# The opening's pair product by channel tiles, all tokens in a step

## The chip, the core and the metric

The kernel runs on one core of a Trainium2 chip. The metric is the device time of one execution in microseconds, as the median of several runs; the profile is of one execution more. The engines have short names: PE (TensorE) multiplies matrices and transposes, ACT (ScalarE) applies functions and copies, DVE (VectorE) does element-wise arithmetic, POOL (GpSimd) here only issues transfers that add into memory, and SP issues the ordinary transfers.

## The reference

A trunk of two layers on x (512 tokens, 1024 channels, float32), each layer a gated feed-forward block, a token mixer, and a second feed-forward block. The change touches the first feed-forward block of the first layer alone:

```python
def rms_norm(x, g):
    y = xf * lax.rsqrt(jnp.mean(xf * xf, axis=-1, keepdims=True) + NORM_EPS)
    return (y * g)
def swiglu(x, w_in, w_out):
    g, u = jnp.split(x @ w_in, 2, axis=-1)          # w_in: 1024 x 5632
    return (jax.nn.silu(g) * u) @ w_out             # w_out: 2816 x 1024
for i in range(DEPTH):                              # DEPTH = 2
    h = h + 0.5 * swiglu(rms_norm(h, ffn1_norm[i]), ffn1_w_in[i], ffn1_w_out[i])
    ...                                             # mixer, then a second feed-forward block
return rms_norm(h, final_norm)
```

## The kernel before

**Products in three parts.** Every operand is split into a high part (`hi`, `whi`) and the rest (`lo`, `wlo`), and a product is made of three matmuls: high by high, low by high, high by low. ACT rounds to the high part (line 96), DVE subtracts to get the rest (line 87; line 93 where a gain is applied at once). Rounded weights lie in four buffers (`whi`, `wlo`), the weights as loaded in eight (`raw`, 1024 columns each).

**The row norm.** The input of the feed-forward block is not divided by its row norm. x is transposed on PE (line 265, tile `e`), multiplied by the channel gain, and used so; the factor `rt` per token is applied to the product, inside the silu and in the product after it. It needs the squares of x (`junk`, ACT), a mean (DVE), a root (ACT) and a Newton step (DVE). The norm is therefore not needed until the first silu.

**Units of x.** x falls into four quarters, A11, A12, A21 and A22 (first digit: tokens 0 to 255 or 256 to 511; second: channels 0 to 511 or 512 to 1023), and each quarter into two groups of 256 channels (`first.g[0]` and `first.g[1]`). A quarter of one group is called a unit here: 256 tokens by 256 channels. A unit is turned by four transposes (`turn`), split (`parts`: two `hi` on ACT, two `lo` on DVE) and kept as a value (`value`) for sums.

**Steps.** The work is a list of steps (`subs`); a step is 12 or 24 matmuls with one weight tile. The list is walked in order (lines 1423 to 1439). Each step has places called pre, mid and rest, before its matmuls, and end and late, after them; `hook(n, place, function)` puts work there. Weights are split some steps ahead, by a table `ahead` in the opening, by three steps later. All instructions of an engine run in the order in which this walk writes them.

**The opening.** Steps 0 to 7 are the pair product, `pair_plain` with `first`: gate and up columns of two blocks (2 x 256 columns) for all tokens, into four PSUM banks (`p`), two for each half of the tokens. Steps 0 to 3 do the first half of the tokens (A12, then A11, a group each), steps 4 to 7 the second half (A22, then A21) with the same four weight tiles of 256 channels by 512 columns, which are held in the four buffers. Silu and the gated product `h` come at steps 7 to 9, which frees the banks. Steps 8 to 21 are the first `chunk` (line 673), a product by a scheme of seven products over quarters and their sums: P1 (A11), P2 (A12), P5 (S1), P6 (S2), P3 (S4), P7 (S3), Q4 (A22), two steps each, into banks A (of `bank`), B (of the pool `aux`) and C. P5, at step 12, is the first to need the two banks C, which the pair product's `h` has to free. `first.rest` puts the sums S1 to S3 and their splits at steps from 5 on. The results are transposed to be the left side of the next product: the pair group's from step 15 on (`left_blocks` with lag 7), the chunk's at the ends of steps 18, 19, 22 and 23. From step 22 on follows the product with w_out (`out_blocks`), whose update is `x<-A,x`.

**Transfers.** SP issues x and the opening's weights: two units of x (256 KB each), the first weight tile in two halves, the second, a quarter of x (512 KB), two weight tiles, two quarters, then the chunk's weights. POOL's adding transfers follow for the weights of P5 and P7.

Of the kernel before, what the change touches and what calls it, by code (L numbers as in the profile page):

```python
# [9 lines left out]
F32R = mybir.dt.float32r  # L10
# [3 lines left out]
P = 128  # L14
# [38 lines left out]
def trunk(ctx: ExitStack, tc: tile.TileContext, a: dict, out: bass.AP):  # L53
# [29 lines left out]
    def f32(t):  # L83
        return t.bitcast(F32)
# [26 lines left out]
    class Raw:  # L111


        halves = False

# [34 lines left out]
    class Sub:  # L150
# [19 lines left out]
        def split(self, vector=False):  # L170

# [549 lines left out]
    def pair_plain(w_in, f0, group, first=False):  # L721


        w, st, ht = 2 * P, {}, {}
        raw = {}
        for k in (1, 0):
            for h in range(2):
                raw[k, h] = PairRaw(w_in, k * 512 + h * 256, f0)
                raws.append(raw[k, h])

        def bank_of(half, s):
            if (half, s) not in st:
                st[half, s] = bank("p")
            return st[half, s]

        def product(sub, half, left, h, between=None):

            sq = [(s, q) for q in range(2) for s in range(2)]
            for i, (s, q, m) in enumerate([(s, q, m) for m in range(3) for s, q in sq] if first and h else
                                          [(s, q, m) for q in range(2) for m in range(3) for s in range(2)] if first else  # L740
                                          [(s, q, m) for s, q in sorted(sq) for m in range(3)]):
                if i == 8 and between is not None:
                    between()
                z = S.z[h].hl[left][m == 1][:, q * H + s * P : q * H + (s + 1) * P]
                nc.tensor.matmul(bank_of(half, s), z, (sub.lo if m == 2 else sub.hi)[:, q, :],  # L745
                                 start=left[2] == "2" and (h, q, m) == (0, 0, 0),
                                 stop=left[2] == "1" and (h, q, m) == (1, 1, 2))

        def silu(half, s):
            t = 2 * half + s  # L750
            ht[t] = slot(name="s1")[:, :w]
            act(ht[t], st[half, s][:, :w], AF.Silu, scale=S.rt[:, t : t + 1])

        def post(half):
            for s in range(2):
                ps, t = st[half, s], 2 * half + s
                if t not in ht:
                    silu(half, s)
                o = slot(name="h")[:, :w]
                stt(o, ps[:, w:], S.rt[:, t : t + 1], ht[t], ALU.mult, ALU.mult)  # L760
                ht[t] = o
            left_blocks(group, ht, half, 7 if first else 2)

        at0 = len(subs)
        for i, (half, left) in enumerate(((0, "A12"), (0, "A11"), (1, "A22"), (1, "A21"))):
            for h in range(2):
                def mm(sub, half=half, left=left, h=h):
                    product(sub, half, left, h, opening["A11"] if first and (left, h) == ("A12", 1) else None)

                end = None  # L770
                if (left, h) == ("A11", 1):
                    end = (lambda: (hook(at0 + 7, "rest", lambda: (silu(0, 0), silu(0, 1))),
                                    hook(at0 + 8, "mid", lambda: post(0)))) if first else lambda: post(0)
                elif (left, h) == ("A21", 1):
                    end = (lambda: hook(at0 + 9, "rest", lambda: post(1))) if first else lambda: post(1)
                subs.append(Sub(raw[1 - i, h], mm, end) if i < 2 else Again(subs[at0 + 2 * (i - 2) + h], mm, end))

    class PairRaw(Raw):


        def __init__(self, w_in, r0, f0):
            super().__init__(None, [P, 2, 512])
            self.w_in, self.r0, self.f0 = w_in, r0, f0

        def fetch(self):
            for q in ((slice(0, 1), slice(1, 2)) if self.halves else (slice(0, 2),)):
                for b, base in enumerate((0, DFF)):
                    c0 = base + self.f0 * P
                    ws = self.w_in[self.r0 + q.start * P : self.r0 + q.stop * P, c0 : c0 + 256]
                    nc.sync.dma_start(out=self.v[:, q, b * 256 : (b + 1) * 256],  # L790
                                      in_=ws.rearrange("(k p) c -> p k c", p=P))

    def ffn(w_in, w_out, norm):
        f0 = 0
        for i, sizes in enumerate(FF_PARTS):
            groups, p0 = [], f0
            for n in sizes:
                if n == "p":
                    groups.append(Group(1))
                    pair_plain(w_in, f0, groups[-1], not subs)  # L800
# [569 lines left out]
    def turn(i, name, where=None):  # L1370
        src, _ = first.src(i, name)
        opening[i, name] = first.g[i].turn(src, where)

    def parts(i, name):
        first.g[i].direct(name, opening[i, name], first.src(i, name)[1])

    def value(i, name, vector=False):

        g, ps, gains = first.g[i], opening.pop((i, name)), first.src(i, name)[1]
        if name == "A21" or not vector:  # L1380
            g.take(name, ps, gains)
            return
# [5 lines left out]
    turn(0, "A12")  # L1388
    warm_up(2, 512)
    turn(1, "A12")  # L1390
    warm_up(2, 512)
    parts(0, "A12")
    subs[0].split()
    parts(1, "A12")
    subs[1].split()
    value(0, "A12")
    value(1, "A12")
    opening["A11"] = lambda: (turn(0, "A11"), turn(1, "A11"))
    for n, phase, fn in ((0, "late", vec_rest),
                         (2, "pre", lambda: (subs[2].split(True), parts(0, "A11"), parts(1, "A11"))),  # L1400
                         (2, "pre", lambda: (subs[3].split(), value(0, "A11", True), value(1, "A11", True))),
                         (2, "end", lambda: (turn(0, "A22", bank), turn(1, "A22", bank))),
                         (3, "pre", lambda: (parts(0, "A22"), parts(1, "A22"))),
                         (3, "mid", lambda: (value(0, "A22"), value(1, "A22", True))),
                         (3, "end", lambda: (turn(0, "A21"), turn(1, "A21"))),
                         (4, "mid", lambda: (parts(0, "A21"), parts(1, "A21"))),
                         (4, "rest", lambda: (value(0, "A21"), value(1, "A21")))):
        hook(n, phase, fn)
    squares(4, "rest", "A11")
# [56 lines left out]
```

## Time and profile before

| | us |
|---|---|
| median of 3 runs | 1625.99 (1625.77 to 1626.8) |
| the profiled execution | 1628.51 |
| its span, first to last instruction | 1626.5 |
| mean granted TensorE clock in it | 0.997 |

| engine | busy us | share of the span | instructions |
|---|---|---|---|
| PE, matmuls | 1611.2 | 99% | 7451 |
| DVE | 1368.9 | 84% | 1830 |
| ACT | 1039.8 | 64% | 1511 |
| POOL | 222.5 | 14% | 201 |

Times in the profile count from the start of the span. A row of a timeline gives the start, the busy time, the engine, the line, the operation with its output and inputs, the shapes, the number of instructions merged into the row, and in brackets the idle time of the engine ahead of it with what ended that. A row of the windows gives the stretch and its length, the busy time of PE, PE's weight loads, DVE, ACT and POOL (with counts), the granted clock, the busy share of the transfer engines and their GB/s. A row of the chain of waits gives start, length and the work that the end of the execution hung on.

### The profile page before, as it was taken

How to read it: one execution, taken by the hardware profiler on the slowest of the kernel's cores; microseconds unless marked ns; L12 is line 12 of the kernel's file. 1: busy time of each engine (PE TensorE's matmuls, PEld its weight loads, DVE VectorE, ACT ScalarE, POOL GpSimd, SP SyncE). 2: the span in 40 equal slices, each digit the busy share in tenths (PEclk: the TensorE clock that was granted, in tenths of full speed). 3: DMA queues.
4: the chain of work that ended last, by engine and by line, in shares of the span. 5: the costliest groups of instructions: out<-in, count | busy, mean ns of one | idle time of the engine just before them, and what ended most of it. 6: DMA issues, size and time to landing. Idle time of an engine off the chain costs nothing.

```text
span 1626.5 us, 20830 instructions
## 1 busy us (share of the span) xinstructions
PE 1611.2 (99%) x7451; PEld 1328.9 (82%) x7451; DVE 1368.9 (84%) x1830; ACT 1039.8 (64%) x1511; POOL 222.5 (14%) x201
## 2 busy tenths in 40 slices
PE   9999999999999999999999999999999999999998
PEld 7888888888878888888888888888888788888886
DVE  6898888887898787877987978878978988879778
ACT  7656556657876656556776565566886765565665
POOL 2111111100010111111101111111211011111110
PEclk9999999999999999999999999999999999999999
DMA  8867876844383786876838778768877557686693
GB/s 273 188 164 166 209 179 158 217 119 115 83 204 84 175 202 162 208 174 158 202 86 190 173 161 211 181 151 209 214 196 193 155 117 195 161 208 162 159 207 99
DMA packets 164551, 279.29 MB, mean 172 GB/s; under 512 B 11504, under 2 KB 37728, under 8 KB 164448
## 3 DMA queue, kind: packets, MB, share of 16 engines
q1 hardware_dynamic: 114944, 184.84, 36.2%
q0 software_dynamic: 47712, 91.30, 33.6%
q10 hardware_dynamic: 1792, 1.84, 0.4%
q8 instruction: 58, 0.95, 0.2%
q14 instruction: 45, 0.37, 0.1%
HBM read 275.84 MB, written 2.10 MB: 171 GB/s over the span
## 4 chain that ended last, share of the span: by engine, by line
PE 90%; DVE 6%; ACT 3%; issue 1%; DMA 1%; SPq 0%; DVEq 0%; ACTq 0%
PE A L365 14%; PE A L366 14%; PE A L367 14%; PE C L366 7%; PE C L367 7%; PE C L365 7%; PE p L745 5%; PE B L365 4%; PE B L367 4%; PE B L366 4%; PE e L265 3%; PE Q L367 1%; PE Q L365 1%; PE Q L366 1%; DVE wlo L87 1%
## 5 line engine op out<-in xcount | busy, mean ns | idle before, releaser
L96 ACT ACTIVATE whi<-raw 128x1024 fp32r<-128x1024 f32 (+1 forms) x536 | 553.0, 1033 | 381.6 <-PE A L366 106.9
L87 DVE TENSOR_TENSOR wlo<-raw,whi 128x1024 fp32r<-128x1024 f32 (+1 forms) x537 | 638.9, 1193 | 182.3 <-ACT whi L96 181.0
L365 PE MATMUL A<-whi,hi 128*128 128x512 f32 x1016 | 405.4, 399 | 1.8 <-DVE x L93 1.8
L366 PE MATMUL A<-whi,lo 128*128 128x512 f32 x1016 | 397.7, 391 | 0.4 <-DVE lo L87 0.3
L367 PE MATMUL A<-wlo,hi 128*128 128x512 f32 x1016 | 397.8, 392 | 0.0
L367 PEld LDWEIGHTS A<-wlo,hi 128*128 128x128 f32 x1016 | 191.3, 188 | 41.7 <-DVE wlo L87 0.3
L366 PEld LDWEIGHTS A<-whi,lo 128*128 128x128 f32 x1016 | 191.7, 189 | 39.5 <-DVE lo L87 1.8
L365 PEld LDWEIGHTS A<-whi,hi 128*128 128x128 f32 x1016 | 191.3, 188 | 39.6 <-ACT whi L96 2.2
L366 PE MATMUL C<-whi,lo 128*128 128x512 f32 x560 | 219.2, 392 | 0.7 <-DVE lo L87 0.5
L365 PE MATMUL C<-whi,hi 128*128 128x512 f32 x560 | 218.8, 391 | 0.0
L367 PE MATMUL C<-wlo,hi 128*128 128x512 f32 x560 | 218.3, 390 | 0.0
L137 POOL DMA_DIRECT2D raw<-in_ffn_w_in_dram x82 | 98.8, 1205 | 741.9 <-DVE raw L87 524.9
L137 POOL DMA_DIRECT2D raw<-in_ffn_w_out_dram x72 | 83.0, 1160 | 378.8 <-DMA raw<-in_ffn_w_out_dram 124.3
L87 DVE TENSOR_TENSOR raw<-raw,raw 128x1024 f32<-128x1024 f32 (+1 forms) x108 | 129.6, 1200 | 1.2 <-DMA raw<-in_ffn_w_out_dram 0.6
L366 PEld LDWEIGHTS C<-whi,lo 128*128 128x128 f32 x560 | 105.2, 188 | 25.3 <-DVE lo L87 3.9
L87 DVE TENSOR_TENSOR lo<-a,hi 128x512 fp32r<-128x512 f32 (+1 forms) x188 | 122.7, 661 | 3.2 <-ACT hi L96 2.8
L96 ACT ACTIVATE hi<-a 128x512 fp32r<-128x512 f32 (+1 forms) x188 | 112.3, 601 | 19.3 <-DVE a L87 15.5
L365 PEld LDWEIGHTS C<-whi,hi 128*128 128x128 f32 x560 | 105.2, 188 | 21.8
L367 PEld LDWEIGHTS C<-wlo,hi 128*128 128x128 f32 x560 | 105.2, 188 | 21.6
L96 ACT ACTIVATE c<-A 128x512 f32<-128x512 f32 x132 | 77.3, 594 | 56.3 <-PE A L367 56.0
L365 PE MATMUL B<-whi,hi 128*128 128x512 f32 x280 | 112.2, 401 | 0.0
L367 PE MATMUL B<-wlo,hi 128*128 128x512 f32 x280 | 109.5, 391 | 0.0
(161 smaller groups left out, 2106.9 us busy)
## 6 DMA issues: line engine op xcount, KB each, us to landing
raw<-in_ffn_w_in_dram SPq DMA_DIRECT2D x162, 512.0 KB, 4.5
raw<-in_ffn_w_out_dram SPq DMA_DIRECT2D x100, 512.0 KB, 5.3
raw<-in_ffn_w_in_dram POOLq DMA_DIRECT2D x82, 512.0 KB, 7.5
raw<-in_ffn_w_out_dram POOLq DMA_DIRECT2D x60, 512.0 KB, 8.0
raw<-in_sg_w_in_dram SPq DMA_DIRECT2D x20, 512.0 KB, 6.6
raw<-in_rec_w_in_dram SPq DMA_DIRECT2D x16, 512.0 KB, 3.9
raw<-in_ffn_w_in_dram SPq DMA_DIRECT2D x30, 256.0 KB, 4.8
raw<-in_sg_w_in_dram POOLq DMA_DIRECT2D x12, 512.0 KB, 7.7
```

What stands on the lines that cost most here:

```text
L87: nc.vector.tensor_tensor(out=o, in0=x, in1=y, op=op)
L96: nc.scalar.activation(out=o, in_=x, func=f, **k)
L137: nc.gpsimd.dma_start(out=self.v, in_=src, accum_op=ALU.add)
L265: nc.tensor.transpose(ps[:, o : o + P], src(q, s), ident)
L365: nc.tensor.matmul(ps, zh, wh, start=fresh and i == 0, stop=False, **k)
L366: nc.tensor.matmul(ps, zl, wh, start=False, stop=False, **k)
L367: nc.tensor.matmul(ps, zh, wl, start=False, stop=end, **k)
L745: nc.tensor.matmul(bank_of(half, s), z, (sub.lo if m == 2 else sub.hi)[:, q, :], start=left[2] == "2" and (h, q, m) == (0, 0, 0), stop=lef ...
```

## The change

The opening's eight steps are written anew (`pair_opening`); other pair products keep the plain order.

- **Order of the product.** Step n takes one tile of 128 channels (tiles 4 to 7, then 0 to 3) for all 512 tokens: six matmuls for the first half of the tokens, six for the second. Each weight tile is 128 channels by 512 columns (256 KB, two transfers) and is used in its step only. So eight weight tiles are split, one each step, where four were held.
- **Order of the loads.** Unit n of x (256 KB) and weight tile n are issued in turn, n from 0 to 7; the units go A12, A22 of the first group, A12, A22 of the second, then A11, A21 of the first and of the second.
- **Inside a step** (`between`). After the first two matmuls of step n come the turn of unit n + 1, its `hi` and `lo`, the split of weight tile n + 1 and the value of unit n - 1. One warm-up pair of matmuls goes.
- **Splits ahead.** `ahead` is 0 to 4 at steps 0 to 4, 6 at step 5, 8 at step 6, 9 at step 7: so at step 6 the splits of weight tiles 7 and 8 (the chunk's first, 1024 columns) are written ahead of that step's `between`.
- **Later work.** Squares move from steps 4 to 6 to steps 5 to 8, the mean and root from step 6 to step 8 and the Newton step from 7 to 9, the four silus to step 9, the four products `h` to step 10, `first.rest` from 1 to 5, so that S1's splits are at steps 9 and 10. The pair group's transposes move from steps 15, 16, 16 and 17 to 17, 18, 19 and 20, and its sums with them from 19, 20 and 21 to 22, 23 and 24.
- **DVE and ACT.** The option that let DVE round a weight tile (line 184) goes; ACT rounds all.

The diff, cut to its core:

```diff
-        def split(self, vector=False):
+        def split(self):
...
-            for q in ((slice(0, 1), slice(1, 2)) if self.raw.halves else (slice(0, k),)):
-                if vector:
-                    nc.vector.tensor_copy(self.hi[:, q, :], src[:, q, :])
-                else:
-                    act(self.hi[:, q, :], src[:, q, :], AF.Copy)
-                tt(self.lo[:, q, :], src[:, q, :], f32(self.hi[:, q, :]), ALU.subtract)
+            act(self.hi, src, AF.Copy)
+            tt(self.lo, src, f32(self.hi), ALU.subtract)
...
+    def pair_opening(w_in, f0, group):
+        ps, ht = {}, {}
+        def mm_of(n, k):
+            def mm(sub):
+                c, h, q = k // 4, k % 4 // 2, k % 2
+                for half in range(2):
+                    name = ("A11", "A12", "A21", "A22")[2 * half + c]
+                    for m in range(3):
+                        for s in range(2):
+                            if n == 0 and m == 0:
+                                ps[half, s] = bank("p")
+                            z = S.z[h].hl[name][m == 1][:, q * H + s * P : q * H + (s + 1) * P]
+                            nc.tensor.matmul(ps[half, s], z, (sub.lo if m == 2 else sub.hi)[:, 0, :],
+                                             start=(n, m) == (0, 0), stop=(n, m) == (7, 2))
+                        if (half, m) == (0, 0):
+                            opening["between"](n)
+            return mm
+        for n, k in enumerate((4, 5, 6, 7, 0, 1, 2, 3)):
+            raws.append(PairRaw(w_in, k * P, f0, 1))
+            subs.append(Sub(raws[-1], mm_of(n, k)))
+        def out(half):
+            for s in range(2):
+                pair_out(ps[half, s], 2 * half + s, ht)
+            left_blocks(group, ht, half, 7 + 2 * half)
+        hook(9, "rest", lambda: [pair_silu(ps[t // 2, t % 2], t, ht) for t in range(TT)])
+        hook(10, "mid", lambda: out(0))
+        hook(10, "rest", lambda: out(1))
...
-    raws[0].halves = True
-    load_x(0, 512, 256)
-    load_x(0, 768, 256)
-    load_more(2)
-    load_x(0, 0)
-    load_more(4)
-    load_x(2, 512)
-    load_x(2, 0)
+    UNITS = [(i, name) for c in (1, 0) for i in range(2) for name in (("A11", "A21"), ("A12", "A22"))[c]]
+    for n, (i, name) in enumerate(UNITS):
+        load_x(QUARTER[name][0], QUARTER[name][1] * 512 + i * 256, 256)
+        load_more(n + 1)
...
+    HOME = (aux, aux, bank, bank, aux, aux, bank, aux)
...
+    def between(n):
+        if n == 0:
+            turn(1)
+            parts(1, 0)
+            subs[1].split()
+            parts(1, 1)
+        elif n < 7:
+            turn(n + 1)
+            parts(n + 1, 0, 1)
+            subs[n + 1].split()
+            value(n - 1)
...
-    squares(4, "rest", "A11")
-    squares(5, "rest", "A12")
-    squares(6, "rest", "A22")
-    squares(6, "rest", "A21")
-    rstd(6, (0, "rest"), (0, "rest"), (1, "pre"))
-    first.rest(1, None)
+    turn(0)
+    warm_up(2, 512)
+    parts(0, 0)
+    subs[0].split()
+    parts(0, 1)
+    hook(0, "late", vec_rest)
+    hook(7, "pre", lambda: value(6))
+    hook(7, "mid", lambda: value(7))
+    squares(5, "late", "A12")
+    squares(6, "late", "A22")
+    squares(7, "rest", "A11")
+    squares(8, "mid", "A21")
+    rstd(8, (0, "mid"), (0, "rest"), (1, "pre"))
+    first.rest(5, None)
...
-    ahead = {0: 1, 1: 1, 2: 3, 3: 3, 4: 3}
+    ahead = {0: 0, 1: 1, 2: 2, 3: 3, 4: 4, 5: 6, 6: 8, 7: 9}
```

More of the change, by code (lines that the diff above doesn't have):

```diff
@@ L727, in pair_plain @@
             for h in range(2):
-                raw[k, h] = PairRaw(w_in, k * 512 + h * 256, f0)
+                raw[k, h] = PairRaw(w_in, k * 512 + h * 256, f0, 2)
                 raws.append(raw[k, h])
[L731 to L752, printed above, removed]
+        def product(sub, half, left, h):
+            for s in range(2):
+                for q in range(2):
+                    for m in range(3):
+                        if (half, s) not in st:
+                            st[half, s] = bank("p")
+                        z = S.z[h].hl[left][m == 1][:, q * H + s * P : q * H + (s + 1) * P]
+                        nc.tensor.matmul(st[half, s], z, (sub.lo if m == 2 else sub.hi)[:, q, :],
+                                         start=left[2] == "2" and (h, q, m) == (0, 0, 0),
+                                         stop=left[2] == "1" and (h, q, m) == (1, 1, 2))
@@ L754, in post @@
         def post(half):
             for s in range(2):
[L756 to L762, printed above, removed]
+                pair_out(st[half, s], 2 * half + s, ht)
+            left_blocks(group, ht, half, 2)
         at0 = len(subs)
@@ L767, in mm @@
                 def mm(sub, half=half, left=left, h=h):
[L768 to L775, printed above, removed]
@@ L1386, in value @@
             ts(t[:, c], ps[:, c], gain, None, ALU.mult)
[L1388 removed]
+    def between(n):
[9 more added lines that the diff above has]
+            value(n - 1)
+    opening["between"] = between
+    turn(0)
     warm_up(2, 512)
[L1390 to L1392 removed]
+    parts(0, 0)
     subs[0].split()
[L1394 to L1408, printed above, removed]
[L1409 to L1414 removed]
+    parts(0, 1)
[8 more added lines that the diff above has]
+    first.rest(5, None)
     hook(20, "end", vec_rest_t)
```

60 lines of the change are left out of this document (40 added, 20 removed).

## The prediction

> **What bounds the kernel now.** I read the page first, then the timelines of PE, ACT and DVE over the first 100 us, the chain of waits there, and the windows.
>
> ```profile
> span 1626.5 us, 20830 instructions
> PE 1611.2 (99%) x7451; PEld 1328.9 (82%) x7451; DVE 1368.9 (84%) x1830; ACT 1039.8 (64%) x1511; POOL 222.5 (14%) x201
> ```
> TensorE is busy for all but 15.3 us of the span, so the opening can pay only through idle time of PE or through where its work starts. PE's timeline (start, busy, group, idle before it and its releaser):
>
> ```profile
> 7.17 0.73 PE L745 MATMUL p<-whi,hi 128*128 128x512 f32 x2 [0.27 <-ACT whi L96]
> 11.05 1.20 PE L745 MATMUL p<-whi,hi 128*128 128x512 f32 x4 [0.87 <-ACT whi L96]
> 16.08 0.73 PE L745 MATMUL p<-whi,lo 128*128 128x512 f32 x2 [0.66 <-DVE lo L93]
> 22.14 1.04 PE L265 MATMUL e<-ident,x 128*128 128x128 f32 x8
> 33.90 0.39 PE L365 MATMUL A<-whi,hi 128*128 128x512 f32 x1
> 36.62 0.39 PE L365 MATMUL A<-whi,hi 128*128 128x512 f32 x1
> 65.49 0.48 PE L365 MATMUL A<-whi,hi 128*128 128x512 f32 x1
> 94.20 0.51 PE L366 MATMUL C<-whi,lo 128*128 128x512 f32 x1 [0.24 <-DVE lo L87]
> ```
> The pair product starts at 7.17 and the first chunk (step 8) at 33.90. The waits between (0.87, 0.66) are PE's last of any size until 94.20, so a microsecond won before 33.90 reaches the end unless a new wait takes it. The chain of waits gives PE's prices:
>
> ```profile
> 22.30 0.87 PE e L265 x8
> 23.17 10.90 PE p L745 x48
> ```
> A pair matmul takes 10.90/48 = 0.227 us, a transpose 0.87/8 = 0.109. A step of the chunk (12 matmuls) takes 36.62 - 33.90 = 2.72.
>
> **The start.** Before, the first weights were queued behind two units of x (512 KB in all); now they come behind one.
>
> ```profile
> 4.73 0.47 SPq L1322 DMA_DIRECT2D x<-in_x_dram  x1
> 4.86 0.84 ACT L96 ACTIVATE hi<-e,vec 128x256 fp32r<-128x256 f32 x2 [1.91 <-PE e L265]
> 6.49 0.63 ACT L96 ACTIVATE whi<-raw 128x512 fp32r<-128x512 f32 x1 [0.79 <-DMA raw<-in_ffn_w_in_dram]
> 5.00:6.00 1.00, 1.00 (x5) 0.76 (x4) 0.27 (x1) 0.70 (x2) 1.00 (x3) 1.00 0.98 312
> 7.00:8.00 1.00, 0.83 (x4) 0.70 (x5) 0.69 (x1) 0.77 (x3) 0.00 (x0) 1.00 0.86 262
> ```
> ACT waited 0.79 us for those weights and split them at 6.49. The 256 KB less ahead of them is worth 0.84 to 1.0 us at 312 to 262 GB/s (the windows' last column); the one issue less on SP is 0.47. More than 1.2 can't be had, since half a unit's `hi` (0.42, from 4.86) stands ahead of the split. So the first product comes 0.47 to 1.2 us earlier; I take 0.87, nearest to the bytes: 6.3. The warm-up pair that goes lay in PE's wait: nothing. The second unit of x now lies where the first weights lay in the stream, so it lands for 6.49 and is wanted at 6.3 + 2 x 0.227 = 6.75.
>
> **The opening on PE without waits.** The work is the same, 96 matmuls and 32 transposes, but 28 transposes instead of 24 lie behind the first product. A step of 12 matmuls and 4 transposes takes 2.72 + 0.44 = 3.16. From 6.3, step 5 starts at 22.1, step 6 at 25.26, and step 8 would at 31.1: 2.8 us before 33.90. That is the whole gain the change can bring, 0.17%.
>
> **ACT from step 5.** ACT works in program order. Its timeline gives each operation's price as the distance to the next start:
>
> ```profile
> 22.77 1.57 ACT L96 ACTIVATE hi<-e,vec 128x256 fp32r<-128x256 f32 x4 [1.00 <-PE e L265]
> 24.21 0.65 ACT L96 ACTIVATE junk<-x 128x512 f32<-128x512 f32 x1
> 24.83 0.65 ACT L96 ACTIVATE junk<-x 128x512 f32<-128x512 f32 x1
> 25.54 1.06 ACT L96 ACTIVATE whi<-raw 128x1024 fp32r<-128x1024 f32 x1
> 26.50 0.62 ACT L96 ACTIVATE hi<-s 128x512 fp32r<-128x512 f32 x1
> 27.03 0.61 ACT L96 ACTIVATE junk<-x 128x512 f32<-128x512 f32 x1
> 32.29 1.28 ACT L96 ACT_TABLE_LOAD   x1
> 33.58 0.20 ACT L96 ACTIVATE ti<-ti 128x4 f32<-128x4 f32 x1
> 40.24 0.83 ACT L96 ACTIVATE s<-p,rt 128x256 f32<-128x256 f32 x2
> 40.95 1.09 ACT L96 ACTIVATE c<-A 128x512 f32<-128x512 f32 x2
> 41.90 1.09 ACT L96 ACTIVATE whi<-raw 128x1024 fp32r<-128x1024 f32 x1
> 42.85 0.65 ACT L96 ACTIVATE hi<-a 128x512 fp32r<-128x512 f32 x1
> ```
> So: a unit's `hi` or its value 0.72 (half of 1.44), a square 0.62, a full weight split 0.95, a half one like a 512 `hi` 0.53, a table load 1.29, two silus 0.71, two copies 0.95. ACT takes up a unit 0.63 after its transposes start (22.14 to 22.77).
>
> In steps 0 to 4 ACT owes `hi`, half split and value, 1.97 of 3.16 us, and DVE as many of its own: no wait. In step 5 ACT takes up unit 6 at 22.1 + 0.45 + 0.63 = 23.2 and from there has no gap: `hi` 0.72, value 0.72, two squares 1.24, split 7 (0.53), split 8 (0.95), and only at 27.35 `hi` of unit 7, whose first half is ready at 27.8. PE wants it at 25.26 + 6 x 0.227 + 0.44 = 27.06. DVE's `lo` of it stands behind `wlo` 8 (from 27.5, 1.14) and is ready at 29.05; PE wants it 0.45 after the `hi`. Step 6 waits 0.75 + 0.8 = 1.5 us, with step 7 queued behind, and step 8 starts at 32.65 instead of 31.1. The splits of 7 and 8, called ahead of the step's own unit, take the place of the waits removed.
>
> ACT goes on from 28.1 (split n + `hi` and so on, in order): five full splits (9 to 13) 4.75, six squares 3.72, two table loads 2.58, value 0.72, root 0.2, one 512 `hi` 0.53, four silus 1.42, two copies 0.95: 43.0. Before, ACT had by 43.5 (the row at 42.85) done all this and four more 512 `hi`, of S2 and S4, which now come later.
>
> **DVE from split 13.**
>
> ```profile
> 43.26 0.87 DVE L93 SCALAR_TENSOR_TENSOR h<-p,rt,s 128x256 f32<-128x256 f32 x2
> 44.04 0.68 DVE L93 SCALAR_TENSOR_TENSOR s<-a,a 128x512 f32<-128x512 f32 x1
> 44.64 1.22 DVE L87 TENSOR_TENSOR raw<-raw,raw 128x1024 f32<-128x1024 f32 x1
> 45.78 1.22 DVE L87 TENSOR_TENSOR wlo<-raw,whi 128x1024 fp32r<-128x1024 f32 x1
> 63.34 0.68 DVE L87 TENSOR_TENSOR c<-C,c 128x512 f32<-128x512 f32 x1
> 64.06 0.75 DVE L93 SCALAR_TENSOR_TENSOR c<-c,rt,c 128x512 f32<-128x512 f32 x1
> 64.73 0.42 DVE L87 TENSOR_TENSOR s<-e,a 128x256 f32<-128x256 f32 x1
> 65.06 1.22 DVE L87 TENSOR_TENSOR wlo<-raw,whi 128x1024 fp32r<-128x1024 f32 x1
> ```
> By distance: `h` 0.39, a 512 operation 0.60, a full one 1.14, a pair of operations on `c` 1.39, a 256 one 0.33. In the new order `wlo` 13 (43.05 to 44.2) stands ahead of the `h` products, which free the pair's PSUM banks; the first bank is free at 44.65. P5 (step 12) takes that bank and would start at 32.65 + 4 x 2.72 = 43.5: a wait of 1.15. Before, even the last `h` was done by 44.04, ahead of P5 at 33.90 + 4 x 2.72 = 44.8. From there DVE has no gap up to the chunk's `c`: one `h` 0.39, `lo` 13 0.60, two `h` 0.78, eight full operations 9.1, eleven 512 ones 6.6, two adds of B 1.2, two pairs on `c` 2.8: 66.1. Before, that ended at 64.73. On the way step 15 waits 0.35 for its `lo`.
>
> **What reaches the end.** PE comes to the transposes of `c`, at the end of step 18, by 32.65 + 11 x 2.72 + 1.15 + 0.35 and four pair-group transposes (0.44) at 64.5, and waits for DVE until 66.1. Three transposes are left, so step 19 starts at 66.5 against 65.49: 1.0 late. Four transposes of the pair group that stood ahead of it now come after it: 1.45. And one of the pair group's block sums (0.33) now falls behind DVE's update at 79.53, into a stretch that DVE fills:
>
> ```profile
> 65.00:70.00 5.00, 5.00 (x28) 4.12 (x27) 3.49 (x7) 4.01 (x8) 0.94 (x1) 1.00 0.89 144
> 79.53 0.69 DVE L93 SCALAR_TENSOR_TENSOR x<-A,x 128x512 f32<-128x512 f32 x1 [0.69 <-PE A L367]
> 85.00:90.00 5.00, 5.00 (x23) 3.95 (x23) 5.00 (x10) 4.40 (x7) 1.69 (x2) 1.00 0.36 52
> ```
> DVE is busy 5.00 of 5.00 us there and PE already waits for it at 94.20, so this passes too: 1.45 + 0.3, about 1.7 us late, and later stages are untouched. The span becomes 1628.2. The profiled run took 1628.51, which is 2.0 over its span and 2.5 over the median, 1625.99; the sum goes onto the median: 1627.7.
>
> **Costs not seen.** SP now issues 24 opening transfers instead of 15, and the chunk's weights wait for them and for a raw buffer. A step needs 0.52 MB in 3.16 us, 166 GB/s; the windows show 262 to 312. I take 0 (between 0 and 1, one late unit of x). POOL's transfers that add to P5's weights wait for split 4 (about 19 us) and are wanted at 37: 0. The long sums can err by 1 us either way.
>
> [...] The row: the table load at 32.29 takes 1.28 and ACT's next instruction starts at 33.58, at once. [...]
>
> **Rivals.** (a) *The gain is kept, wholly or in part*: ACT reaches unit 7 in time, or its and DVE's queues run a few per cent shorter than the rows. With all 4.5 us of waits gone 1626.0 - 2.8 = 1623.2, with half of them 1625.4. For it: before, the same work hid behind PE up to 94.20; against: it has less time now. (b) *Slower: DVE's backlog outlasts 79.53.* All five moved operations of the pair group (5 x 0.33) fall behind it, and `c` is 1 us later than 66.1: 1.45 + 1.65 + 1.0 = 4.1, 1630.1. It decides from `c` at 67 on. For it: 5.00 of 5.00; against: 1.5 us to spare from 65 to 70. (c) *Slower: the transfers set the opening's pace.* It decides below 166 GB/s; at half of what the windows show, 0.66 us in each of the five steps ahead of unit 6: 1.7 + 3.3, 1631.0. The rows of 262 and 312 speak against it, with transfers of the same size in flight. [...]
>
> **How the numbers follow.** A measurement of this kernel can tell about 0.2%, 3.25 us. The forecast, 1625.5 to 1629.2, likeliest 1627.7: 0.55. (a), 1623.2 to 1625.5: 0.28. More than 2.8 us isn't in the change: over 0.2% faster 0.02. (b) 0.09, (c) 0.04, (d) 0.02: slower by over 0.2% 0.15. Within 0.2%: 0.83. The range, 1623.3 to 1630.3, leaves out the end of (a) and half of (b) to (d).
>
> **What would show it.** Right: the first product near 6.3; in step 6 PE waits for `hi` (ACT) and `lo` (DVE), 1.5 together; the chunk starts near 32.7; C waits for DVE's `h` near 43.5; the transposes of `c` wait for DVE to 66. Wrong: none of these waits and each stage 2.8 ahead: (a). Waits for DMA in steps 1 to 7: (c). A stall at 94 that is more than 1 us longer: (b).

## The result and the profile after

| | before | after |
|---|---|---|
| median, us | 1626.65 (6 runs) | 1631.65 (6 runs, 1631.09 to 1633.42) |
| profiled execution, us | 1628.51 | 1631.28 |
| its span, us | 1626.5 | 1629.6 |

The ratio of times is 1.0034, with a 95% interval of 1.0024 to 1.0044: the change makes the kernel 0.34% slower, 5.5 us in the means (which the ratio compares), 5.0 in the medians and 3.1 between the two traces. The forecast was 1627.7 (1623.3 to 1630.3).

The head of the profile after: TensorE is busy within 0.7 us as long as before, and 2.4 of the 3.1 us are time in which it waits.

```profile
span 1629.6 us, 20853 instructions
PE 1611.9 (99%) x7449; PEld 1327.0 (81%) x7449; DVE 1367.5 (84%) x1830; ACT 1042.1 (64%) x1517; POOL 222.4 (14%) x201
```

PE's timeline of the changed kernel, at the places that the prediction named (start, busy, group, idle before it and its releaser):

```profile
6.27 0.73 PE L775 MATMUL p<-whi,hi 128*128 128x512 f32 x2 [0.32 <-ACT whi L96]
...
14.92 0.62 PE L775 MATMUL p<-whi,hi 128*128 128x512 f32 x2
15.60 0.73 PE L775 MATMUL p<-whi,lo 128*128 128x512 f32 x2
...
29.17 0.74 PE L775 MATMUL p<-whi,hi 128*128 128x512 f32 x2 [0.58 <-ACT hi L96]
30.46 0.73 PE L775 MATMUL p<-whi,lo 128*128 128x512 f32 x2 [0.55 <-DVE lo L93]
...
46.31 0.47 PE L358 MATMUL C<-whi,hi 128*128 128x512 f32 x1 [1.04 <-DVE h L93]
...
67.67 0.55 PE L258 MATMUL e<-ident,c 128*128 128x128 f32 x3 [1.00 <-DVE c L93]
67.97 0.48 PE L358 MATMUL A<-whi,hi 128*128 128x512 f32 x1
```

The first product, the two waits of step 6, the bank wait at C and the wait at the transposes of `c` all stand in the places that were forecast, the later ones 1.4 to 1.7 us late (the forecast wait at C would have ended at 44.65). New is the pair at 15.60, in step 2: 0.68 us behind the pair before it instead of 0.46. ACT and DVE show why, and how the queue goes on:

```profile
14.19 0.84 ACT L96 ACTIVATE hi<-e,vec 128x256 fp32r<-128x256 f32 x2 [1.11 <-PE e L258]
...
27.17 1.58 ACT L96 ACTIVATE whi<-raw 128x512 fp32r<-128x512 f32 x2
28.64 0.84 ACT L96 ACTIVATE hi<-e,vec 128x256 fp32r<-128x256 f32 x2
...
43.42 1.09 ACT L96 ACTIVATE whi<-raw 128x1024 fp32r<-128x1024 f32 x1
```

```profile
15.06 0.88 DVE L93 SCALAR_TENSOR_TENSOR lo<-e,vec,hi 128x256 fp32r<-128x256 f32 x2 [1.73 <-ACT hi L96]
...
44.55 1.22 DVE L87 TENSOR_TENSOR wlo<-raw,whi 128x1024 fp32r<-128x1024 f32 x1 [1.76 <-ACT whi L96]
45.69 0.87 DVE L93 SCALAR_TENSOR_TENSOR h<-p,rt,s 128x256 f32<-128x256 f32 x2
...
66.86 0.75 DVE L93 SCALAR_TENSOR_TENSOR c<-c,rt,c 128x512 f32<-128x512 f32 x1
...
72.59 1.22 DVE L87 TENSOR_TENSOR wlo<-raw,whi 128x1024 fp32r<-128x1024 f32 x1 [1.97 <-ACT whi L96]
...
111.44 1.28 DVE L93 SCALAR_TENSOR_TENSOR x<-Q,x 128x512 f32<-128x512 f32 x2
```

The first `lo` (15.06) starts only when both `hi` are done (14.19 + 0.84), though the first `hi` was done at about 14.67 (a single one takes 0.48). Step 6's `hi` stands behind the splits of weight tiles 7 and 8 (27.17), `h` behind split 13 and its rest (44.55).

**A mark that is worth more than the times.** In the kernel before, the same update of x from Q came at 108.19, in a second trace of it at 107.69:

```profile
108.19 1.30 DVE L93 SCALAR_TENSOR_TENSOR x<-Q,x 128x512 f32<-128x512 f32 x2
```

Behind this mark every kernel here runs alike: the rest of the span is 1516.6 to 1517.3 us in ten of the traces below and 1517.8 to 1518.3 in eight. The eight are those with a stretch of half speed near 477 us (granted clock 0.50 in the windows of before below), which costs 1.1 us in the mean and lies far behind the change (last section). So the mark prices a change of the opening to about half a microsecond in one trace (two traces of one kernel differ by 0.50 and 0.37), as long as no stretch of half speed lies ahead of it. By it the change costs 3.25 us, and 3.25 to 4.1 between any two traces of the two kernels.

### The profile page after: what moved, and what is told of

Its sections match the earlier page's. It is cut to its first block, busy times and chain, and to the rows that moved or that the text cites. A ratio compares the mean times of both kernels' runs of the same rounds, so it can differ in the third digit from the quotient of the medians.

```text
span 1629.6 us, 20853 instructions
## 1 busy us (share of the span) xinstructions
PE 1611.9 (99%) x7449; PEld 1327.0 (81%) x7449; DVE 1367.5 (84%) x1830; ACT 1042.1 (64%) x1517; POOL 222.4 (14%) x201
## 3 DMA queue, kind: packets, MB, share of 16 engines
q10 hardware_dynamic: 1792, 1.84, 0.4%
## 4 chain that ended last, share of the span: by engine, by line
PE 92%; DVE 4%; ACT 2%; DMA 1%; issue 1%; SPq 0%; DVEq 0%; ACTq 0%
PE A L358 14%; PE A L359 14%; PE A L360 14%; PE C L359 7%; PE C L360 7%; PE C L358 7%; PE p L731 4%; PE B L358 4%; PE B L360 4%; PE B L359 4%; PE e L258 3%; PE r L218 2%; PE r L216 2%; PE r L217 2%; PE Q L358 1%; PE Q L360 1%
```

## The experiments

Theory of the queues: the loss is a chain. TensorE loses time in the steps (waits for `lo`), so ACT gets to the last units late; ACT works without a gap from 24.5 us, then DVE from 45, and what stands late in them (`h`, `c`) is waited for. Rivals: TensorE's own waits add up without the queues; DVE's total work decides alone; the transfers set the pace. In the table T0 is the first product, T8 the first chunk step, mark the update of x from Q.

| run | T0 | T8 | wait at C | wait at `c` | mark | ratio to before (interval) |
|---|---|---|---|---|---|---|
| before, two traces | 7.17, 6.72 | 33.90, 33.39 | 0 | 0 | 108.19, 107.69 | |
| changed, two traces | 6.27, 6.34 | 34.23, 34.67 | 1.04, 1.03 | 1.00, 1.00 | 111.44, 111.81 | 1.0034, 1.0029 |
| e1 half by half | 6.65 | 36.47 | 0.82 | 1.00 | 113.45 | 1.0033 (1.0021 to 1.0046) |
| e2 splits behind unit | 6.36 | 34.65 | 2.81 | 0 | 113.64 | 1.0033 (1.0021 to 1.0044) |
| e3 four squares early | 5.98 | 32.42 | 0.58 | 0.99 | 109.19 | 1.0013 (1.0004 to 1.0022) |
| e4 eight squares early | 6.57 | 33.10 | 0 | 1.00 | 109.17 | 1.0013 (1.0005 to 1.0022) |
| e5 late part alone | 6.78 | 32.87 | 0.78 | 0.88 | 109.19 | 1.0012 (1.0004 to 1.0021) |
| e6 e4, pair's end and sums earlier | 6.93 | 34.97 | 0 | 0 | 109.20 | 1.0004 (0.9995 to 1.0013) |
| e8 four warm-ups | 6.74 | 34.40 | 1.04 | 1.00 | 111.58 | 1.0021 (1.0012 to 1.0030) |
| e9 e4, pair's end earlier | 6.04 | 34.16 | 0 | 1.00 | 109.84 | 1.0009 (1.0000 to 1.0018) |
| e10 e4, sums earlier | 6.62 | 35.03 | 0 | 0 | 109.37 | 1.0003 (0.9994 to 1.0012) |
| e11 e6, e8, two tiles | 6.55 | 33.44 | 0 | 0 | 108.71 | 1.0007 (0.9999 to 1.0016) |
| e12 two banks | 6.32 | 34.23 | 1.04 | 1.00 | 111.45 | 1.0027 (1.0017 to 1.0037) |
| e13 together | 6.36 | 32.23 | 0 | 0 | 108.26 | 1.0001 (0.9992 to 1.0010) |
| e14 no warm-up | 6.59 | 36.19 | 1.00 | 1.00 | 113.36 | 1.0021 (1.0012 to 1.0031) |
| e15 sums late, in before | 7.20 | 33.81 | 0 | 0.23 | 108.20 | 1.0000 (0.9991 to 1.0008) |

**Both kernels again.** 

> The kernel before, unchanged, for a second trace. If the first profiled execution of it was an untypical one (1628.51 against medians of 1625.99 and 1626.65), the new trace has a span near 1624.6 and some stage after the opening in which it is about 2 us ahead of the first trace; then the change costs 5.0 us, of which 3.1 lie ahead of 120 us. If the offset between profiled and other executions belongs to the kernel, the span comes out near 1626.5 again and the 1.9 us between the traces (3.1) and the medians (5.0) stay open. The ratio of times shows what no change looks like: 1.000 within 0.0005.

> The changed kernel, unchanged, for a second trace and more times. The update of x from Q within 0.6 us of 111.44 (the landing of the first x differs by 0.3 between traces). If the distance between the traces (3.1) and the medians (5.0) comes from stretches in which TensorE's granted clock falls to half for about 3.5 us behind one of its waits (seen near 477 us in both traces of before and near 481 in the changed kernel's, 1.2 to 1.5 us each), the executions fall into groups about 1.4 us apart, and the changed kernel's lie in the later groups more often than those of before. If not, its times form one group near 1631.3. The ratio again 1.0034 (1.0024 to 1.0044).

Before against itself: 0.9995 (0.9986 to 1.0004), mark 107.69. The changed kernel again: 1.0029 (1.0018 to 1.0039), mark 111.81. Both traces of before have the stretch of half speed near 477 us, the changed kernel's first trace has it, its second does not:

```profile
475.00:476.00 1.00, 0.00 (x0) 0.00 (x0) 0.93 (x2) 1.00 (x3) 0.00 (x0) 1.00 0.85 180
476.00:477.00 1.00, 0.49 (x2) 0.48 (x3) 1.00 (x3) 0.97 (x3) 0.00 (x0) 1.00 0.83 238
477.00:478.00 1.00, 1.00 (x4) 0.81 (x4) 1.00 (x1) 1.00 (x2) 0.00 (x0) 0.66 0.64 244
478.00:479.00 1.00, 1.00 (x4) 0.71 (x4) 1.00 (x3) 0.84 (x2) 0.00 (x0) 0.50 0.01 4
```

These are windows of the kernel before (busy time of PE, its loads, DVE, ACT and POOL, then the granted clock): PE stands still, and then runs four matmuls in a microsecond where others have six. That the changed kernel falls into this stretch more often than before was expected; the times are too spread to show groups, so it is neither confirmed nor excluded.

**Why `lo` waits.** e1 finishes each unit half by half:

```diff
-            parts(n + 1, 0, 1)
+            parts(n + 1, 0)
+            parts(n + 1, 1)
```

> The changed kernel with each unit's first half finished (hi and lo) before the second half's hi is called. Theory of the queues (ScalarE from 24.5 to 45 us and VectorE from 45 to 68 have no gap, and everything in them hangs on when the unit-6 transposes come): steps 2 and 4 take 3.21 instead of 3.54, step 5 starts 0.66 earlier (22.7), step 8 0.7 to 1.1 earlier, and the queues move with it: 0.7 us at the end, 1631.0, ratio to the kernel before 1.0030. Rival, the transfers pace the opening: the steps keep their lengths, nothing at the end. Rival, VectorE's total work up to 68 us decides alone: the steps are shorter, but the transposes of c still start at 67.7.

The even steps did shorten, to 3.29, but ACT's second `hi` now waited for DVE's first `lo`, in step 6 for so long that PE waited 1.46 there instead of 0.58; behind that wait PE ran at half clock for about 3.4 us (granted 0.51, 0.50, 0.50 and 0.79 in the four windows of a microsecond from 32 to 36), and step 8 came at 36.47. ACT's timeline of e1:

```profile
20.93 0.48 ACT L96 ACTIVATE hi<-e,vec 128x256 fp32r<-128x256 f32 x1 [0.53 <-PE e L258]
21.95 0.47 ACT L96 ACTIVATE hi<-e,vec 128x256 fp32r<-128x256 f32 x1 [0.55 <-DVE lo L93]
```

So the program lets only one of the two engines at a time work on a unit, because of the tile that both halves are written to, or because of the PSUM bank that both read. e11 gave the halves of units 3, 5 and 7 tiles of their own, e12 (on the changed kernel) two PSUM banks to unit 3 and one to unit 5:

```diff
+            g.hl[name] = ([Halves([slot(F32R, x) for _ in range(2)]) for x in ("hi", "lo")] if n in (3, 5, 7) else ...)  # e11
+        opening[n] = Halves([bank("e"), aux("e")])                                     # e12, n == 3
```

> Squares, pair's end and sums early, four warm-up matmuls, and units 3, 5 and 7 with a tile for each half of hi and lo, finished half by half. If a lo waits for both hi because the two halves share a tile, steps 2 and 4 now take 3.2 to 3.25 instead of 3.54, without the wait of ScalarE for VectorE that half by half brought in one tile; step 5 starts 16.5 behind the first product instead of 17.1, step 8 at 25.9 instead of 26.5 behind it, and the update of x from Q comes near 106.6: the first version ahead of before, ratio 0.9992 (0.9982 to 1.0002). Rival, the halves wait for each other whatever tiles they are in, or other operations wait for the six more slots: steps 2 and 4 at 3.54 or longer, update at 107.2 or later.

> The changed kernel with unit 3 turned into two PSUM banks (one for each half) and unit 5 into one as before; both are finished half by half, hi and lo in one tile each. If ScalarE and VectorE are kept from reading one PSUM bank at the same time, the second hi of unit 3 follows the first at once and its first lo starts beside it, while the second hi of unit 5 waits about 0.55 us for the first lo; steps 2 and 4 both take 3.2 to 3.3. If the shared tile is what they wait on, unit 3's second hi waits as unit 5's does. The time is that of the changed kernel less about 0.5: ratio 1.0028 (1.0018 to 1.0038).

In e11 the second `hi` waited as in e1 (0.55 in step 4, 1.33 in step 6). In e12's ACT timeline unit 3's two `hi` (13.77) follow each other without a gap, DVE's first `lo` starting at 14.28 beside the second; unit 5's (20.60, 21.63) don't:

```profile
13.77 0.84 ACT L96 ACTIVATE hi<-e,vec 128x256 fp32r<-128x256 f32 x2 [0.91 <-PE e L1402]
...
20.60 0.48 ACT L96 ACTIVATE hi<-e,vec 128x256 fp32r<-128x256 f32 x1 [1.10 <-PE e L258]
21.63 0.48 ACT L96 ACTIVATE hi<-e,vec 128x256 fp32r<-128x256 f32 x1 [0.55 <-DVE lo L93]
```

So it is what they read and not what they write: the PSUM bank, or the tile `e` that lies in it (two banks were also two tiles; no run puts two tiles into one bank). In one bank the second `hi` waited 0.55 for the first `lo`, in two it did not wait. Steps 2 and 4 took 3.22 and 3.20; but step 5's transposes came late (step 5 took 3.90; the rearranged banks are the likely cause, the trace names none), so the mark (111.45) gained nothing.

**Which queue.** e2 calls the splits behind unit 7, e3 and e4 call squares in steps 1 to 4, e4 the root at step 7 too:

```diff
-    ahead = {..., 4: 4, 5: 6, 6: 8, 7: 9}
+    ahead = {..., 4: 4, 5: 5, 6: 6, 7: 9}                         # e2
-    squares(5, "late", "A12"); squares(6, "late", "A22")
+    squares(3, "late", "A12"); squares(4, "late", "A22")          # e3; e4: all eight in steps 1 to 4
```

> The changed kernel with the weight splits 7 and 8 called behind unit 7's hi and lo, as in the steps before, instead of ahead of them. Every theory: the two waits of step 6 (0.58 and 0.55) go, step 8 starts near 33.1 instead of 34.2. Theory of the queues: ScalarE has as much to do from 24.5 to 45 as before, so split 13 and the h products come when they came (45.7), the bank wait grows from 1.04 to 2.1 and the end is the same within 0.3 us: ratio 1.0034. Rival, TensorE's waits in the opening reach the end by themselves: 1.1 us less, ratio 1.0027.

> The changed kernel with four of the eight squares (2.4 us of ScalarE) called in steps 3 and 4, where ScalarE is busy 2.4 of 5 us, instead of steps 5 and 6. Theory of the queues: split 13 comes at about 41.0 instead of 43.4, the h products at 43.3 instead of 45.7, no bank wait at the first C product, step 6 waits 0.5 instead of 1.13, the transposes of c start 1.5 to 2.4 us earlier (65.3 to 66.2), and the end is 1.5 to 2.4 us earlier: ratio 1.0020 to 1.0025. Rival, TensorE's waits in the opening decide: only step 6's part comes back, 0.6. Rival, VectorE's total work decides: c ends at 67.6 as before and nothing comes back.

> The changed kernel with all eight squares called in steps 1 to 4 (into the steps whose value is VectorE's, three each in steps 2 and 4) and the root one step earlier (step 7). Theory of the queues: ScalarE's stretch without a gap from 24.5 us loses 4.9 us of work; step 6 waits for nothing, step 8 starts near 32.2, split 13 comes near 40, the h products near 41.5, no bank wait at the first C product, the transposes of c wait for VectorE 0.3 or less; the first update of x from Q (111.44 us in the changed kernel, 108.19 and 107.69 in two traces of before) comes near 107.6 and the ratio is 1.000 (0.9990 to 1.0010). Rival, VectorE's backlog behind 45 us stands on the moved work of the pair group and of the first norm and not on ScalarE: the transposes of c still wait 1.0 and the update comes near 109.0, as with four squares.

e2: step 6 waits for nothing, and the wait turns up at C, 2.81 instead of 1.04:

```profile
48.58 0.77 PE L358 MATMUL C<-whi,hi 128*128 128x512 f32 x1 [2.81 <-DVE h L93]
```

(Its mark is 2.2 late; step 5 already started 1.76 late, by the half speed told of below.) Less that, the mark is 0.4 late where the rival wanted it 1.1 early: TensorE's waits are not added up at the end, the queue is. e3 takes 2.4 us out of that queue and brings 2.25 at the mark (0.3 of it by an earlier first product); the wait at C became 0.58 and did not go. e4 takes out as much again and the mark stays, though its first product came 0.59 later than e3's: the C wait is gone, but the transposes of `c` wait 1.00 as before. ACT's and PE's timelines of e4:

```profile
35.84 1.06 ACT L96 ACTIVATE whi<-raw 128x1024 fp32r<-128x1024 f32 x1 [1.06 <-PE A L359]
```

```profile
65.39 0.55 PE L258 MATMUL e<-ident,c 128*128 128x128 f32 x3 [1.00 <-DVE c L93]
```

There the theory's ACT part failed and the rival on DVE's stretch was right: ACT no longer works without a gap, it waits 1.06 for step 8's matmuls before its next split, DVE's stretch starts when it did in e3 (42.26, 42.28) and takes as long (22.32) up to its last operation on `c`.

**DVE's stretch.** On e4, e9 calls the pair's silus, `h` and blocks one step earlier, e10 the first norm's sums two steps earlier, e6 both. e5 and e15 go the other way, from the kernel before: all later places of the change, or the sums alone.

```diff
-        hook(9, "rest", silus); hook(10, "mid", out(0)); hook(10, "rest", out(1))
+        hook(8, "mid", silus);  hook(9, "mid", out(0));  hook(9, "rest", out(1))     # e6, e9
-    first.rest(5, None)
+    first.rest(3, None)                                                              # e6, e10
-    first.rest(1, None)                                                              # in before:
+    first.rest(5, None)                                                              # e5, e15
```

> The kernel before with its own opening product and load order, but with the change's later places for the squares, the root, the silus, the h products, the sums of the first norm and the pair group's blocks. Theory of the queues: ScalarE starts that work as before (from 22 us), but the h products and the sums fall behind split 13 and into VectorE's stretch from 43 us; no bank wait at the first C product, the transposes of c wait about 0.6, and four pair-group transposes and a sum come after them: the update of x from Q comes 1.3 us later than before (109.2), ratio 1.0008 (1.0004 to 1.0013). Rival, the later places are the whole loss and the order of the opening none: the update comes near 111.4, ratio 1.0025 or more. Rival, they cost nothing by themselves: 107.9, ratio 1.0000.

> The kernel with all eight squares early, and the pair's silus, h products and blocks one step earlier and the first norm's sums two steps earlier. Theory of the queues: what is left of VectorE's backlog goes, one step's pair-group transposes come back ahead of c: the update of x from Q near 107.2 (106.7 to 107.6), ratio 0.9995 (0.9985 to 1.0005), the first version that is not behind the kernel before. Rival, TensorE's own steps (3.54 in the even steps, 1.3 us in all) hold the rest: the same as with the squares alone.

> All eight squares early, and only the pair's silus, h products and blocks one step earlier; the first norm's sums where the change has them. From step 8 to the update of x from Q it took 76.07 us with the squares alone and 74.23 with the pair's end and the sums both earlier (74.29 and 74.30 in the traces of before). If the pair group's moved transposes and sum are the loss: 74.6 or less, and no wait at the transposes of c. If the first norm's sums and their parts in VectorE's stretch behind 45 us are: 76 and a wait of 1.0. My expectation is between, 75.1, with a wait of about 0.5; ratio 1.0008.

> All eight squares early, and only the first norm's sums two steps earlier; the pair's end where the change has it. The counterpart of the run before: if the sums are the loss, 74.6 or less from step 8 to the update of x from Q, and no wait at the transposes of c; if the pair group's moved work is, 76. My expectation: 75.1; ratio 1.0008.

> The kernel before with one edit: the first norm's sums and their parts four steps later, where the change has them. All later places together cost it 1.0 to 1.5 us (update of x from Q at 109.19 against 108.19 and 107.69). If the sums carry that, as in the changed kernel (1.73 of 1.84): a wait of about 0.9 at the transposes of c and the update 1.0 to 1.5 later than before, ratio 1.0008 (1.0000 to 1.0016). If the pair's end does: no wait there and 1.0000.

From step 8 to the mark it took 76.07 us in e4, 75.68 in e9, 74.34 in e10 and 74.23 in e6 (before: 74.29). The last three compare best, since step 8 was late in all of them (half speed in step 0, below): of 75.68 the sums' places take 1.45 off, and with them the wait at `c` goes; the pair's end is worth 0.1 to 0.4, and e9 kept the wait at 1.00. My even split was wrong. DVE's stretch says the same: from its last wait to the last operation on `c` it is 22.32 in e4 (42.26 to 64.58) and 20.02 in e10 (44.19 to 64.21). At the mark itself e6 and e10 are no earlier than e4 (109.20 and 109.37 for 109.17), since their step 8 was 1.9 late; their gain shows in the distance and, with intervals that overlap, in the ratios. In the kernel before the later sums cost nothing (e15): its DVE waits twice between 50 and 60 us (0.69 and 0.51), and in e15 these waits are gone. PE's timeline of e15:

```profile
65.24 0.55 PE L265 MATMUL e<-ident,c 128*128 128x128 f32 x3 [0.23 <-DVE c L93]
```

Only all later places together cost it something, 1.0 to 1.5 at the mark (e5), with the waits of the changed kernel: 0.78 at C, which I had not expected, and 0.88 at `c`.

**The warm-up pair.** 

> The changed kernel with four warm-up matmuls instead of two behind the first transposes, as many as the kernel before has there; TensorE waits there in any case. In three traces of the changed opening (splits behind the unit, pair's end early, and partly the changed kernel's second trace) the first pair of matmuls took 1.22 us instead of 0.73 and step 0 up to 1.7 us longer, TensorE having waited 0.35 to 1.25 before it: half speed. If that comes from the wait ahead of the first product, the longer warm-up takes it away: first pair 0.73, update of x from Q near 111.2, the late group of times (spans from 1631) rarer, ratio 1.0027 (1.0020 to 1.0034). Rival, half speed there does not hang on the warm-up: times as those of the changed kernel, ratio 1.0031.

> The changed kernel without warm-up matmuls behind the first transposes (none instead of two). If they decide whether step 0 runs at full speed, its matmuls run at half speed in nearly every execution: first pair 1.22 us, step 0 up to 1.7 us longer, spans 1630 to 1632, ratio 1.0039 (1.0029 to 1.0049), against 1.0034 and 1.0029 with two and 1.0021 with four. Rival, the difference between two and four was chance: as the changed kernel.

PE's timeline of e14 and of e8, the first product:

```profile
6.59 1.22 PE L775 MATMUL p<-whi,hi 128*128 128x512 f32 x2 [1.77 <-ACT whi L96]
```

```profile
6.74 0.73 PE L775 MATMUL p<-whi,hi 128*128 128x512 f32 x2 [0.76 <-ACT whi L96]
```

In four of ten traces with two warm-up matmuls (e2, e6, e9, e10), and in e14 with none, step 0's matmuls start at half speed (first pair 1.22 us, the next two 1.00 apart; in the changed kernel's first trace 0.73 and 0.55) and step 0 takes 4.9 to 5.3 us; in the three with four (e8, e11, e13) 3.3. The second trace of the changed kernel had less of it (first pair 1.22, step 0 3.97); its first trace took 3.62 with a first pair of 0.73, so that need not be the same. A trace can lose up to 1.9 us there. That the number of warm-ups decides it is not shown: three traces with four are few, and four and none came out alike in the ratio, 1.0021, against my 1.0039 for none, with intervals that reach the 1.0029 of two. Nor does it happen in nearly every execution without warm-ups: e14's traced one has its mark at 113.36 and a span of 1630.2, but four of its ten have spans of 1627.9 to 1628.3, less than such a mark and the shortest rest (1516.6) add up to. What it costs a mean execution stays open.

**All together.** e13 is e6 with four warm-ups, units 3 and 5 half by half and the splits behind unit 7.

> What the runs so far point to, together: all eight squares early, the pair's end one step and the first norm's sums two steps earlier, four warm-up matmuls, units 3 and 5 half by half, and the splits 7 and 8 behind unit 7. Steps 0 to 7 then take 3.33, 3.2, 3.2, 3.25, 3.25, 3.25, 3.54 and 2.73, 25.75 in all; with the first product at 6.5 and 74.2 from step 8 on, the update of x from Q comes at 106.5, 1.2 to 1.7 us ahead of the two traces of before: ratio 0.9992 (0.9982 to 1.0001), the first version ahead of it. If what is saved in the opening is again taken by VectorE's stretch up to the transposes of c, a wait of 0.5 to 1.0 stands there and the update comes near 107.3: ratio 0.9998.

The opening did what was expected: step 8 25.87 us behind the first product (27.96 in the changed kernel), at 32.23. The mark is 108.26, no better than before, and the ratio 1.0001. PE's timeline of e13 shows where part of the forecast 1.2 to 1.7 us went:

```profile
46.65 0.50 PE L360 MATMUL C<-wlo,hi 128*128 128x512 f32 x1 [0.21 <-DVE wlo L87]
50.12 0.50 PE L360 MATMUL A<-wlo,hi 128*128 128x512 f32 x1 [0.47 <-DVE wlo L87]
...
53.66 0.50 PE L360 MATMUL A<-wlo,hi 128*128 128x512 f32 x1 [0.48 <-DVE wlo L87]
```

and DVE's timelines, of e13 first and then of e6, show why:

```profile
39.12 0.69 DVE L87 TENSOR_TENSOR lo<-s,hi 128x512 fp32r<-128x512 f32 x1 [1.22 <-ACT hi L96]
...
64.16 0.75 DVE L93 SCALAR_TENSOR_TENSOR c<-c,rt,c 128x512 f32<-128x512 f32 x1
```

```profile
40.08 0.69 DVE L87 TENSOR_TENSOR lo<-s,hi 128x512 fp32r<-128x512 f32 x1 [1.23 <-ACT hi L96]
...
65.12 0.75 DVE L93 SCALAR_TENSOR_TENSOR c<-c,rt,c 128x512 f32<-128x512 f32 x1
```

In e13 DVE last waited at 39.12 and has no gap up to its last operation on `c`, 25.04 us later; in e6, where step 8 came 2.74 later, the same stretch was 40.08 to 65.12, again 25.04. It starts when ACT has split what the last units bring: in e13 ACT works from 27.05 to 43 with one gap, of 0.72, and the splits of weight tiles 7 and 8, 1.47 us, now stand in that stretch, behind unit 7's `hi`. So of 2.74 us at step 8 only 0.96 reached `c`, and 0.94 the mark (109.20 to 108.26). An earlier start of TensorE is worth little here unless these stretches of ACT and DVE move, and no version was shown to run ahead of the kernel before.

## Why the prediction was wrong, point by point

- **The start**: 6.27 for 6.3, right, but not to the digit: the other traces of this opening and its variants had 5.98 to 6.93, by the landing of the first transfers (ACT waited 0.63 for the first weights in e1, 0.35 in e2 and not at all in the changed kernel's first trace, where PE had waited 0.22 for the first unit of x). That the warm-up pair costs nothing is not settled (above).
- **A step without waits, 3.16, and no wait in steps 0 to 4**: the odd steps took 3.20. The even ones did not: this is the step that failed. The sum compared the work of ACT and of DVE with the length of a step, and let the first `lo` run beside the second `hi`; but the two read the same bank and come one after the other (in step 2 the second `hi` ends at 15.03, the first `lo` starts at 15.06), and in the even steps PE wants that `lo` in the same step. Step 5 started 1.3 later than worked out (23.39, not 22.1), 0.77 of it in steps 2 and 4 (3.54 and 3.55), 0.46 in step 0 (3.62). That this went through to the end is read from the trace, where all that follows is late by as much; the runs that shortened the even steps alone lost the gain to other waits (e1, e12).
- **Transfers and the table load**: PE, ACT and DVE wait for no DMA in steps 1 to 7, and rival (c) is out; ACT went on 1.29 us after a table load of 1.28 started, at both loads (36.74 and 39.73), and no run shows ACT held any longer at a load, which is what (d) supposes. (The 0.66 us a step of rival (c) does not come out of its rates: half of 312 and of 262 GB/s make 0.2 and 0.84.)
- **ACT from step 5, DVE from split 13**: right. Step 6 waited 1.13 for a forecast 1.5, C 1.04 for 1.15, the transposes of `c` 1.00 for 1.6; the operations came in the order worked out, all 1.3 to 1.7 later.
- **What reaches the end**: 3.25 at the mark for a forecast 1.75. Step 19 started at 67.97, 2.48 later than before, for a forecast 1.0; behind it another 0.77 was lost, for a forecast 0.75. So that part was right, and the miss lies ahead of step 19, where the 1.3 of step 5 came in. Rival (b) has its condition (`c` at 67.6, it decides from 67 on) and nearly its price, but not its mechanism: DVE waits again at 72.59, long before 79.53, and the wait of 0.24 that stood at 94.20 stands at 97.42 and is still 0.24.
- **Onto the median**: the second step that failed. The sum put a loss worked out in one trace onto the median. The traced execution of before lay 1.86 above its median of six (1628.51, 1626.65), the changed kernel's 0.37 below its own, so the medians are 5.0 apart and the traced executions 2.8 (their spans 3.1). Both traces have the stretch at 477 us, so that stretch isn't the reason. Besides, the median of three that the sum went onto, 1625.99, was 0.66 low. Span against span the miss is 1.4 (1629.6 for 1628.2); against the medians 3.95.
- **Open**: the marks explain 3.3 to 4.1 us of the 4.4 to 5.0 in the medians. The rest is about as much as one stretch of half speed, near 477 us or in step 0; that either comes more often in the changed kernel was not shown.

Rival (a) was right in one thing, that queues can be mended: with squares and sums in other places no loss can be told any more (e10: 1.0003, 0.9994 to 1.0012). Its gain of 2.8 isn't there, as e13 shows.

## What to carry to other kernels

Before counting on an earlier start, follow the engines behind it to the next stretch in which one of them has no gap: what such a stretch does not need sooner is worth little, and what is put into it can cost its full length. When two engines read the halves of one PSUM bank, look in a trace whether they take turns, as here (0.55 us of waiting in e12's one bank), and then count them one after the other. To price a change of a tenth of a per cent, compare the time of a mark behind the change in several traces, and not only the total.

## What the runs showed of the hardware

- Near 477 us PE stands still for much the same time in these traces: 1.84 us in both of before, 1.92 in the changed kernel's first, 1.87 in e3. In 8 of the 18 traces, the first three of these among them, half clock follows, for 3.4 us (before: granted 0.66, 0.50, 0.50 and 0.64 in the four windows from 477 to 481); in the other ten, e3's among them, it does not. e2's wait of 2.81 at C was followed by half clock as well, again for 3.4 us (granted 0.55, 0.50, 0.50 and 0.75 from 48 to 52); two of these windows of e2:

```profile
49.00:50.00 1.00, 1.00 (x4) 0.72 (x4) 1.00 (x3) 0.00 (x0) 0.00 (x0) 0.50 0.00 0
50.00:51.00 1.00, 1.00 (x4) 0.82 (x3) 1.00 (x3) 0.00 (x0) 0.00 (x0) 0.50 0.00 0
```

It did not show at the mark: from C's start to the mark it took 65.06 us, in the changed kernel 65.13, and the wait of 1.00 at `c` was gone.
- In step 0 of e14 the granted clock stands at 1.00 in the windows while the matmuls are slow: the pairs start 1.00 and 0.85 apart (8.32, 9.32, 10.17), in e8 the same pairs 0.55 and 0.47. There only the durations tell. The window of e14:

```profile
9.00:10.00 1.00, 1.00 (x4) 0.81 (x3) 0.75 (x2) 0.97 (x3) 0.00 (x0) 1.00 0.97 303
```
